# A recurrent layer in a four-layer model: elementwise steps on GpSimd, shared slots, output projections behind all blocks

## The chip, the cores and the metric

The kernel is one program on one core of a Trainium2 chip. A core has five engines that run side by side and wait for one another through semaphores: TensorE (PE: matrix products, with PEld for its weight loads), VectorE (DVE), ScalarE (ACT), GpSimd (POOL) and SyncE (SP, which issues the DMAs here). Each engine works through its own instructions strictly in the order in which they stand. The metric is the time of one execution in microseconds; less is better.

## The reference

The model has four layers; each is a mixer and an MLP, both followed by a layer normalization, on 256 tokens of 1024 channels in float32. Layers 0 and 3 mix by retention, layer 2 by latent attention, and layer 1 by the recurrence that the change is about:

```python
gate_branch, rec = jnp.split(x @ w_in, 2, axis=-1)          # 1024 -> 2 x 1280
gate_branch = jax.nn.gelu(gate_branch)
u = conv_general_dilated(rec, conv_w, ...) + conv_b         # 4 taps along the tokens
r = sigmoid(einsum(ub, w_a) + b_a); i = sigmoid(einsum(ub, w_x) + b_x)   # 10 blocks of 128 channels
log_a = -8 * r * softplus(-lam);  a = exp(log_a)
b_in = sqrt(-expm1(2 * log_a)) * (i * u)
h[t] = a[t] * h[t-1] + b_in[t]                              # a scan along the tokens
return (h * gate_branch) @ w_o                              # 1280 -> 1024
```

## The kernel before

Everything is kept transposed where it can be: channels on the 128 partitions, the 256 tokens along them. A float32 product is made of three products of float32r parts: a value is split into a high part (`hi`, a cast on ScalarE, line 140) and the rest (`lo`, a subtraction on VectorE, line 141). That holds for weights too: a chunk of 1 MB comes by DMA into a tile `raw` (3 slots) and is split into a tile `hl` (5 slots), so each chunk costs two casts of 128x1024 on ScalarE and two subtractions of that size on VectorE. `Feed` loads two chunks ahead of use.

The recurrent layer is the function `lru`. It treats its 1280 channels as five blocks `n` of 2x128. For each block:

- `block` and `rows` (TensorE) make the recurrent input in PSUM; `conv` (ScalarE line 569, VectorE line 571) makes `U[n]`, and its split `uT`.
- `gates(n)` multiplies by the gate weights, and ScalarE takes tanh and exp into `tr`, `ti` and `e0`, which have one slot each (lines 583 to 586): the next block's tanh can overwrite `ti` only when the readers of this block's are done. Four steps on VectorE follow: `B` (587), `Q` (588), `B` + 1 (589), `U` scaled by `ti` (590).
- `roots(n)` (line 604, ScalarE) takes the square root of `Q[n]`; all five stand together so that the activation table is loaded once.
- `scan(n)` (VectorE): `U*Q` (line 609), then two scans of 256 tokens (line 611), one for each 128 channels.
- `gate_branch(n)` (TensorE) makes the other half of the input product; `finish(n)` takes its gelu (ScalarE, 619), multiplies by the scan's result (VectorE, 620) and splits the product into `yT[n]` (lines 140 and 141).
- `out(n)` (line 155) multiplies `yT[n]` by a chunk of `w_o` into four PSUM accumulators.

The source before scans all five blocks, finishes blocks 0 and 1, issues `gate_branch` 3 and 4, then `out(0)`, `finish(2)`, `out(1)`, `finish(3)`, `finish(4)`; `close` makes `out` 2 to 4 and the layer normalization. The order on each engine is not that of the source: a scheduler goes over the instructions by priority and writes a fixed order for each engine, which the rows below the diff show. GpSimd does one thing in the kernel before: the power -0.5 of one column in `rstd` (line 162), 36 times.

Of the kernel before, what the change touches and what calls it, by code (L numbers as in the profile page):

```python
# [31 lines left out]
def constants():  # L32
    """Tables that depend on shapes alone."""
    c = {}
    c["c_idn"] = np.eye(128, dtype=np.float32)
    p = np.arange(128, dtype=np.float32)
    c["c_inv"] = np.stack(
        [np.float32(10000.0) ** (-p / np.float32(128)),
         np.float32(10000.0) ** (-(p % 32) / np.float32(32)),
         np.where((p // 32) % 2 == 0, -1.0, 1.0)], -1).astype(np.float32)  # L40
    j = np.arange(128, dtype=np.float64)[:, None]
    i = np.arange(256, dtype=np.float64)[None, :]
    dec = np.zeros((128, RH, 384), np.float64)
    for h in range(RH):
        lg = np.log1p(-np.exp2(-5.0 - h))
        full = np.where(i >= j, np.exp(lg * np.maximum(i - j, 0.0)), 0.0) * RDK ** -0.5
        dec[:, h, 128:] = full
        dec[:, h, :128] = full[:, :128]
    c["c_dec"] = dec.reshape(128, RH * 384).astype(np.float32)
    tri = np.where(np.arange(128)[None, :] <= np.arange(128)[:, None], 0.0, -1e30)  # L50
    c["c_msk"] = np.concatenate([np.zeros((128, 128)), tri, tri], 1).astype(np.float32)
    return c


def packed(w, k, n):
    """w [.., rows, cols] -> [.., rows / 128k, cols / n, 128, k, n]: each piece that is loaded at once in one stretch."""
    *b, r, c = w.shape
    w = w.reshape(*b, r // (128 * k), k, 128, c // n, n)
    m = len(b)
    return w.transpose(*range(m), m, m + 3, m + 2, m + 1, m + 4)  # L60


def laid_out(i):
    """The inputs as the kernel reads them; only the order of the weights' elements changes."""
    a = {n: i[n] for n in _PLAIN}
    w = i["ret_w_in"]
    a["ret_qk"] = packed(w[:, :, :2048], 8, 256)
    a["ret_vg"] = packed(w[:, :, 2048:], 4, 512)
    a["ret_o"] = packed(i["ret_w_o"], 2, 1024)
    a["lru_in"] = packed(i["lru_w_in"][0], 8, 256)  # L70
    a["lru_a"], a["lru_x"] = (i[n][0].transpose(1, 0, 2) for n in ("lru_w_a", "lru_w_x"))
    a["lru_o"] = packed(i["lru_w_o"][0], 2, 1024)
    a["mla_in"] = packed(i["mla_w_in"][0], 2, 704)
    a["mla_uq"] = packed(i["mla_w_uq"][0], 3, 384)
    a["mla_ukv"] = packed(i["mla_w_ukv"][0], 2, 1024)
    a["mla_o"] = packed(i["mla_w_o"][0], 2, 1024)
    w = i["mlp_w1"]
    a["mlp_1a"] = packed(w[:, :, :512], 4, 512)
    a["mlp_1b"] = packed(w[:, :, 512:], 8, 256)
    a["mlp_2"] = packed(i["mlp_w2"], 2, 1024)  # L80
    return {n: np.ascontiguousarray(x) for n, x in a.items()}


class Feed:
    """Weight tiles in the order of their use, each begun some tiles ahead of it."""

# [10 lines left out]
class Model:  # L97
# [13 lines left out]

# [1 line left out]
    def work(self):  # L113
# [6 lines left out]
    def chunk(self, src, k, n, pieces=2, loads=1, hold=True, mid=None):  # L120
        """src [128, k, n] in DRAM -> a tile [128, 2, k, n]: its high and low parts."""
        nc = self.nc
        raw = self.raw.tile([128, 2048], F32, name="raw", tag="raw")
        hl = self.hl.tile([128, 2, 2048], F32R, name="hl", tag="hl")
        w = k * n
        src = src.rearrange("p k n -> p (k n)")
        step = w // loads
        for a in range(0, w, step):
            nc.sync.dma_start(out=raw[:, a:a + step], in_=src[:, a:a + step])
            if mid and a == 0:  # L130
                mid()
        step = w // pieces
        for a in range(0, w, step):
            lo = self.split(hl[:, 0, a:a + step], hl[:, 1, a:a + step], raw[:, a:a + step])
            if hold and self.hold:
                self.after(lo, self.hold)
        return hl[:, :, :w].rearrange("p s (k n) -> p s k n", n=n)
# [5 lines left out]
    def mm3(self, out, st, mv, start, stop):  # L143
        """out += st @ mv with st, mv = (high, low)."""
        mm = self.nc.tensor.matmul
# [4 lines left out]
    def proj(self, acc, t, st, w, k, first, last, ns=(0, 1)):  # L150
        """acc[t] += st.T @ w[:, :, k]; st = (high, low) [128, 128 tokens], 1024 columns."""
        mm = self.nc.tensor.matmul
# [11 lines left out]

# [1 line left out]
    def setup(self):  # L166
# [23 lines left out]
    def vectors_load(self):  # L190
        """The vectors that are used by channel: rows of 128, turned into columns later."""
        nc, A = self.nc, self.A
# [100 lines left out]
    def close(self, acc, gb, final, emits, first=None):  # L293
        """The last products of a phase, each emit(t, ns), and its normalization.

        emits is for both token tiles, or for the second where first is for the other."""
        for t in range(2):
# [15 lines left out]
    def flush(self):  # L313
        """The second token tile of xT, after what the first alone allows."""
        if self.pending:
            self.hold = self.to_xT(1)
        self.pending = False

# [1 line left out]
    def rope2(self, p, ps, out):  # L320
        """ps [128, (x1 | x2), 256] in PSUM -> out [128, 2, (r1 | r2), 256], high and low."""
        nc = self.nc
# [8 lines left out]
    def ret(self, l, final, first=False):  # L331
# [4 lines left out]
        with tc.tile_pool(name="ret", bufs=1) as p:  # L336
# [25 lines left out]
            def begin():  # L362
                """The values of the first head, in the order in which the inputs arrive."""
                ps = [self.work() for t in range(2)]
# [123 lines left out]

# [1 line left out]
    def lru_setup(self, cols):  # L490
# [32 lines left out]
    def lru(self, l, final):  # L523
# [5 lines left out]
        with tc.tile_pool(name="lru", bufs=1) as p:  # L529
            UT, GB, YT = {}, {}, {}  # L530
            U = [p.tile([128, 2, 256], F32, name=f"U{n}") for n in range(5)]
            Q = [p.tile([128, 2, 256], F32, name=f"Q{n}") for n in range(5)]
            B = [p.tile([128, 2, 256], F32, name=f"B{n}") for n in range(5)]
            last = {}
# [40 lines left out]
            def gates(n, w, off):  # L575
# [11 lines left out]
                stt(out=B[n], in0=e0, scalar=1.0, in1=tr, op0=ALU.add, op1=ALU.mult)  # L587
                stt(out=Q[n], in0=B[n], scalar=2.0, in1=B[n], op0=ALU.add, op1=ALU.mult)
                nc.vector.tensor_scalar_add(out=B[n], in0=B[n], scalar1=1.0)
                stt(out=U[n], in0=ti, scalar=1.0, in1=U[n], op0=ALU.add, op1=ALU.mult)  # L590

# [16 lines left out]
            def scan(n):  # L608
                nc.vector.tensor_mul(out=U[n], in0=U[n], in1=Q[n])
                for b in range(2):  # L610
# [6 lines left out]
            def finish(n):  # L617
                g = p.tile([128, 2, 256], F32, name="gg", tag="gg", bufs=2)
                self.after(act(out=g, in_=GB[n], func=AF.Gelu_apprx_tanh), last["s"])
                nc.vector.tensor_mul(out=g, in0=g, in1=Q[n])  # L620
                YT[n] = p.tile([128, 2, 2, 256], F32R, name="yT", tag="yT", bufs=3)
                self.split(YT[n][:, 0], YT[n][:, 1], g)
# [39 lines left out]
            for n in range(5):  # L662
                roots(n)
            for n in range(5):
                scan(n)
                if n < 2:
                    finish(n)
            gate_branch(3, w)
            gate_branch(4, feed(("b", 4)))
            acc = self.accs()  # L670
            gb = self.ln_load(l, 0)
            for n in range(2):
                w = feed(("o", n))
                out(n, w, 0)
                out(n, w, 1)
                finish(n + 2)
            finish(4)
            self.close(acc, gb, final, [lambda t, ns, n=n: out(n, feed(("o", n)), t, ns) for n in (2, 3, 4)])

# [1 line left out]
    def mla(self, l, final):  # L681
# [6 lines left out]
        with tc.tile_pool(name="mla", bufs=1) as p:  # L688
# [13 lines left out]
            def down(t, i):  # L702
                """A latent of a token tile, normalized; with the first its rotary key."""
                c = slice(t * 128, t * 128 + 128)
# [34 lines left out]
            def tables():  # L739
                """Cosines and signed sines by token."""  # L740
                ps = self.work().rearrange("p (t a i) -> p t a i", t=2, a=2)
# [5 lines left out]
            def swapped(dst, src):  # L747
                """dst, src [128, k, r, 64]; the halves of the last axis trade places."""
                f = nc.scalar.copy if dst[1] == 0 else nc.vector.tensor_copy
# [3 lines left out]
            def rope(out, ps):  # L753
                """ps [128, (plain | swapped), 256] in PSUM."""
                a = p.tile([128, 2, 256], F32, name="ra", tag="ra")
# [25 lines left out]
            def q_load(n):  # L781
                """Columns of a pair of heads: (plain | swapped) rotary parts apart from the others."""
                raw = self.raw.tile([128, 2048], F32, name="raw", tag="raw")[:, :1152]
# [120 lines left out]

# [1 line left out]
    def mlp(self, l, final):  # L906
# [120 lines left out]
```

## Time and profile before

| | |
|---|---|
| median of 3 runs | 1343.36 us (1343.08 to 1346.11) |
| span of the profiled execution | 1343.4 us |
| TensorE busy | 1327.7 us, 99% |
| VectorE, ScalarE, GpSimd busy | 960.0, 663.8, 25.9 us |
| recurrent layer, first product to last | about 388 to 492 us of the span |

The profiled execution's span and the median of the runs are the same to 0.1 us, so nothing of note lies around the span. A busy TensorE is not a TensorE at its peak, but its products stand back to back; where it is idle is where time can be won, and where other engines can come to be waited for. The granted clock (PEclk) is given as a share of full speed.

### The profile page before, as it was taken

To read this page: it belongs to the slowest core of one execution; us is meant where nothing else is said; L and a number is where in the kernel's file an instruction comes from. 1 tells how busy PE (TensorE), PEld (TensorE's weight loads), DVE (VectorE), ACT (ScalarE), POOL (GpSimd) and SP (SyncE) were. 2 spreads that over 40 slices of the span, in tenths; PEclk is the share of its full clock that TensorE was granted. 3 is DMA by queue.
4 is the path that set the end of the run, shared out by engine and by line. 5 is a ranking of instruction groups with operands and counts; after the bars stand their busy time and mean duration, and the time that the engine had idled before them with its cause. 6 is when DMAs were issued, how large, how long until landed. Compare 5 with 4: busy or idle time off the path is not lost.

```text
span 1343.4 us, 18112 instructions
## 1 busy us (share of the span) xinstructions
PE 1327.7 (99%) x7184; PEld 1137.0 (85%) x7184; DVE 960.0 (71%) x1498; ACT 663.8 (49%) x1032; POOL 25.9 (2%) x40
## 2 busy tenths in 40 slices
PE   9999999999999999999999999999999999999997
PEld 7888888888889978888888888888898888888886
DVE  6986678666678988666688786666787657876664
ACT  5654345544438855444366454444354445454440
POOL 0000000000000000000000000000000000000000
PEclk9999999999999999999999999999999999999999
DMA  7754544655543456555354265555465444465530
GB/s 289 269 177 175 188 157 184 224 188 188 188 162 130 168 209 251 189 188 188 118 171 171 81 225 212 186 189 185 164 214 185 173 175 163 153 241 190 186 130 32
DMA packets 37426, 243.59 MB, mean 181 GB/s; under 512 B 4328, under 2 KB 4829, under 8 KB 10333
## 3 DMA queue, kind: packets, MB, share of 16 engines
q1 hardware_dynamic: 37340, 242.43, 50.4%
q8 instruction: 56, 0.92, 0.3%
q14 instruction: 30, 0.24, 0.1%
HBM read 241.36 MB, written 1.05 MB: 180 GB/s over the span
## 4 chain that ended last, share of the span: by engine, by line
PE 92%; DVE 4%; ACT 2%; issue 1%; DMA 0%; POOL 0%; SPq 0%; DVEq 0%; POOLq 0%; ACTq 0%
PE acc L155 36%; PE wk L933 14%; PE wk L146 11%; PE wk L148 10%; PE wk L147 10%; PE wk L934 7%; DVE hl L141 1%; PE wk L262 1%; ACT hl L140 1%; PE wk L424 1%; PE wk L955 0%; DVE Q L611 0%; ACT e L585 0%; DMA idn<-c_idn 0%; ACT tr L583 0%
## 5 line engine op out<-in xcount | busy, mean ns | idle before, releaser
L141 DVE TENSOR_TENSOR hl<-raw,hl 128x1024 fp32r<-128x1024 f32 (+2 forms) x450 | 523.1, 1192 | 196.7 <-ACT hl L140 193.6
L140 ACT CAST hl<-raw 128x1024 fp32r<-128x1024 f32 (+2 forms) x450 | 443.0, 1028 | 330.7 <-PE acc L155 191.9
L155 PE MATMUL acc<-hl,hT 128*128 128x512 f32 x1536 | 367.5, 395 | 0.0
L155 PEld LDWEIGHTS acc<-hl,hT 128*128 128x128 f32 x1536 | 285.4, 188 | 64.5
L933 PE MATMUL wk<-xT,hl 128*128 128x512 f32 x832 | 295.4, 398 | 0.0
L934 PE MATMUL wk<-xT,hl 128*128 128x256 f32 x832 | 233.3, 280 | 0.0
L933 PEld LDWEIGHTS wk<-xT,hl 128*128 128x128 f32 x832 | 156.3, 188 | 37.8
L146 PE MATMUL wk<-hl,xT 128*128 128x512 f32 (+1 forms) x432 | 158.8, 368 | 0.3 <-ACT xT L140 0.3
L934 PEld LDWEIGHTS wk<-xT,hl 128*128 128x128 f32 x832 | 157.1, 189 | 1.9
L148 PE MATMUL wk<-hl,xT 128*128 128x512 f32 (+1 forms) x432 | 157.3, 364 | 0.0
L147 PE MATMUL wk<-hl,xT 128*128 128x512 f32 (+1 forms) x432 | 157.1, 364 | 0.0
L155 PE MATMUL acc<-hl,yT 128*128 128x512 f32 x504 | 122.3, 400 | 2.5 <-ACT yT L140 2.2
L155 PEld LDWEIGHTS acc<-hl,yT 128*128 128x128 f32 x504 | 95.1, 191 | 26.3 <-ACT yT L140 2.7
L146 PEld LDWEIGHTS wk<-hl,xT 128*128 128x128 f32 x432 | 81.9, 190 | 14.7 <-ACT xT L140 2.6
L148 PEld LDWEIGHTS wk<-hl,xT 128*128 128x128 f32 x432 | 81.6, 189 | 14.0 <-DVE xT L141 1.6
L147 PEld LDWEIGHTS wk<-hl,xT 128*128 128x128 f32 x432 | 81.9, 190 | 12.9 <-DVE hl L141 1.0
L924 ACT COPY tb<-wk 128x256 f32<-128x256 f32 x104 | 38.8, 373 | 91.8 <-PE wk L934 91.8
L148 PE MATMUL wk<-xT,hl 128*128 128x256 f32 x288 | 81.6, 284 | 0.1
L146 PE MATMUL wk<-xT,hl 128*128 128x256 f32 x288 | 81.5, 283 | 0.0
L147 PE MATMUL wk<-xT,hl 128*128 128x256 f32 x288 | 81.4, 283 | 0.0
L925 DVE TENSOR_TENSOR s<-wk,tb 128x256 f32<-128x256 f32 x104 | 43.7, 420 | 45.6 <-ACT tb L924 45.5
L140 ACT CAST hT<-q 128x256 fp32r<-128x256 f32 x104 | 42.3, 407 | 50.7 <-DVE q L926 50.7
(218 smaller groups left out, 1391.8 us busy)
## 6 DMA issues: line engine op xcount, KB each, us to landing
raw<-mlp SPq DMA_DIRECT2D x64, 1024.0 KB, 4.8
raw<-mlp_1b SPq DMA_DIRECT2D x56, 1024.0 KB, 4.8
raw<-ret_vg SPq DMA_DIRECT2D x30, 1024.0 KB, 5.0
raw<-ret_qk SPq DMA_DIRECT2D x16, 1024.0 KB
raw<-ret_o SPq DMA_DIRECT2D x16, 1024.0 KB, 4.9
raw<-lru_in SPq DMA_DIRECT2D x10, 1024.0 KB, 4.8
raw<-mlp_1a SPq DMA_DIRECT2D x8, 1024.0 KB
raw<-lru_o SPq DMA_DIRECT2D x5, 1024.0 KB, 4.8
```

The costliest lines, as they stand in the source:

```text
L140: self.nc.scalar.copy(out=hi, in_=x)
L141: return self.nc.vector.tensor_sub(out=lo, in0=x, in1=hi.bitcast(F32))
L146: mm(out, lhsT=st[0], rhs=mv[0], start=start, stop=False)
L147: mm(out, lhsT=st[0], rhs=mv[1], start=False, stop=False)
L148: mm(out, lhsT=st[1], rhs=mv[0], start=False, stop=stop)
L155: mm(acc[t][n], lhsT=st[a], rhs=w[:, b, k, n * 512:n * 512 + 512], start=first and i == 0, stop=last and i == 2)
L262: nc.tensor.transpose(ps[:, k * 128:k * 128 + 128], self.h[t][:, (j * 4 + k) * 128:(j * 4 + k + 1) * 128], self.idn)
L424: nc.tensor.transpose(tp[:, b * 128:b * 128 + 128], Y[h, t][:, b * 128:b * 128 + 128], self.idn)
L924: nc.scalar.copy(out=tb, in_=ps_lo)
L925: nc.vector.tensor_add(out=s, in0=ps_hi, in1=tb)
L933: mm(ps, lhsT=w[:, 0, k, b * 128:b * 128 + 128], rhs=xT[:, k], start=k == 0, stop=False)
L934: mm(ps[:, 256:], lhsT=w[:, 1, k, b * 128:b * 128 + 128], rhs=xT[:, k, 0], start=False, stop=k == 7)
```

## The change

The steps on `Q`, `B`+1, `U` and the product `U*Q` go from VectorE to GpSimd. GpSimd has no combined step of two operations here, so what were four instructions on VectorE (588, 589, 590, 609) are six on GpSimd: `ti`+1, `U*ti`, `B`+2, `Q*B`, `B`+1, and `U*Q`. `U` and `B` become the two halves of one tile with the tag `UB` in five slots, and `yT` takes its slots from the same five. `finish` is called for all blocks before the first `out`. Docstrings and comments go too, which shifts line numbers by 3 in the second half of the file. The diff, cut to its code:

```diff
@@ lru @@
-            U = [p.tile([128, 2, 256], F32, name=f"U{n}") for n in range(5)]
+            UB = [p.tile([128, 2, 2, 256], F32, name="UB", tag="UB", bufs=5) for n in range(5)]
+            U, B = [x[:, 0] for x in UB], [x[:, 1] for x in UB]
             Q = [p.tile([128, 2, 256], F32, name=f"Q{n}") for n in range(5)]
-            B = [p.tile([128, 2, 256], F32, name=f"B{n}") for n in range(5)]
...
                 stt(out=B[n], in0=e0, scalar=1.0, in1=tr, op0=ALU.add, op1=ALU.mult)
-                stt(out=Q[n], in0=B[n], scalar=2.0, in1=B[n], op0=ALU.add, op1=ALU.mult)
-                nc.vector.tensor_scalar_add(out=B[n], in0=B[n], scalar1=1.0)
-                stt(out=U[n], in0=ti, scalar=1.0, in1=U[n], op0=ALU.add, op1=ALU.mult)
+                pool = nc.gpsimd
+                pool.tensor_scalar_add(out=Q[n], in0=B[n], scalar1=2.0)
+                pool.tensor_mul(out=Q[n], in0=Q[n], in1=B[n])
+                pool.tensor_scalar_add(out=ti, in0=ti, scalar1=1.0)
+                pool.tensor_mul(out=U[n], in0=U[n], in1=ti)
+                pool.tensor_scalar_add(out=B[n], in0=B[n], scalar1=1.0)
...
             def scan(n):
-                nc.vector.tensor_mul(out=U[n], in0=U[n], in1=Q[n])
+                nc.gpsimd.tensor_mul(out=U[n], in0=U[n], in1=Q[n])
...
-                YT[n] = p.tile([128, 2, 2, 256], F32R, name="yT", tag="yT", bufs=3)
+                YT[n] = p.tile([128, 2, 2, 256], F32R, name="yT", tag="UB", bufs=5)
...
-            for n in range(5):
+            for n in range(3):
                 scan(n)
-                if n < 2:
-                    finish(n)
+                finish(n)
             gate_branch(3, w)
             gate_branch(4, feed(("b", 4)))
+            for n in (3, 4):
+                scan(n)
+                finish(n)
             acc = self.accs()
             gb = self.ln_load(l, 0)
             for n in range(2):
                 w = feed(("o", n))
                 out(n, w, 0)
                 out(n, w, 1)
-                finish(n + 2)
-            finish(4)
```

On VectorE, at the end of the gates, before (`Q0` to `Q4`, `U0` to `U4` and `B0` to `B4` are the five blocks', the two `gg` are blocks 0 and 1):

```order
L589 TENSOR_SCALAR B4_3405<-B4_3405 128x512
L609 TENSOR_TENSOR U0_3391<-U0_3391,Q0_3396 128x512
L609 TENSOR_TENSOR U1_3392<-U1_3392,Q1_3397 128x512
L611 SCALAR_TENSOR_TENSOR Q0_3396<-B0_3401,U0_3391 128x256 x2
L611 SCALAR_TENSOR_TENSOR Q1_3397<-B1_3402,U1_3392 128x256 x2
L609 TENSOR_TENSOR U2_3393<-U2_3393,Q2_3398 128x512
L609 TENSOR_TENSOR U3_3394<-U3_3394,Q3_3399 128x512
L620 TENSOR_TENSOR gg_4143<-gg_4143,Q0_3396 128x512
L620 TENSOR_TENSOR gg_4152<-gg_4152,Q1_3397 128x512
L611 SCALAR_TENSOR_TENSOR Q2_3398<-B2_3403,U2_3393 128x256 x2
L141 TENSOR_TENSOR yT_4146<-gg_4143,yT_4146 128x512
L141 TENSOR_TENSOR yT_4155<-gg_4152,yT_4155 128x512
```

The same place of the changed kernel, where `UB_3391` to `UB_3395` hold `U` and `B` of blocks 0 to 4:

```order
L587 SCALAR_TENSOR_TENSOR UB_3395<-e0_4048,tr_4046 128x512
L141 TENSOR_TENSOR hl_4134<-raw_4133,hl_4134 128x1024 x2
L614 SCALAR_TENSOR_TENSOR Q0_3396<-UB_3391 128x256 x2
L614 SCALAR_TENSOR_TENSOR Q1_3397<-UB_3392 128x256 x2
L614 SCALAR_TENSOR_TENSOR Q2_3398<-UB_3393 128x256 x2
L614 SCALAR_TENSOR_TENSOR Q3_3399<-UB_3394 128x256 x2
L614 SCALAR_TENSOR_TENSOR Q4_3400<-UB_3395 128x256 x2
L623 TENSOR_TENSOR gg_4148<-gg_4148,Q0_3396 128x512
L623 TENSOR_TENSOR gg_4157<-gg_4157,Q1_3397 128x512
L141 TENSOR_TENSOR hl_4222<-raw_4221,hl_4222 128x1024
L141 TENSOR_TENSOR yT_4151<-gg_4148,yT_4151 128x512
L141 TENSOR_TENSOR yT_4160<-gg_4157,yT_4160 128x512
```

Before, the products for blocks 0 and 1 stand behind two blocks' scans; now they stand behind the scans of all five, and a weight chunk's subtraction stands between them and `yT`.

On GpSimd, in the same layer, the rows of the last block's gates and the five products (there are five rows like the first five for each of the blocks 0 to 3 ahead of these; before there is no row on GpSimd here):

```order
L591 TENSOR_SCALAR ti_4047<-ti_4047 128x512
L592 TENSOR_TENSOR UB_3395<-UB_3395,ti_4047 128x512
L589 TENSOR_SCALAR Q4_3400<-UB_3395 128x512
L590 TENSOR_TENSOR Q4_3400<-Q4_3400,UB_3395 128x512
L593 TENSOR_SCALAR UB_3395<-UB_3395 128x512
L612 TENSOR_TENSOR UB_3391<-UB_3391,Q0_3396 128x512
L612 TENSOR_TENSOR UB_3392<-UB_3392,Q1_3397 128x512
L612 TENSOR_TENSOR UB_3393<-UB_3393,Q2_3398 128x512
L612 TENSOR_TENSOR UB_3394<-UB_3394,Q3_3399 128x512
L612 TENSOR_TENSOR UB_3395<-UB_3395,Q4_3400 128x512
```

The first product of any block stands behind the gate steps of all of them. TensorE's order differs in the layer only in how the gate products are laid among the other blocks' products; SyncE's order is the same in both kernels.

## Rows read from the trace of the kernel before

**Rows 1.** Busy time of each engine, its share of the span, instructions (the page).
```profile
PE 1327.7 (99%) x7184; PEld 1137.0 (85%) x7184; DVE 960.0 (71%) x1498; ACT 663.8 (49%) x1032; POOL 25.9 (2%) x40
```

**Rows 2.** TensorE's waits in the whole span: us in total, times, longest.
```profile
PE acc L155 <- ACT yT L140: 2.2, 1, 2.2
PE wk L833 <- DVE s L828: 1.5, 1, 1.5
...
PE acc L155 <- DVE yT L141: 0.3, 1, 0.3
```

**Rows 3.** Busy time by stretch: PE, PEld, DVE, ACT, POOL, granted clock, DMA.
```profile
422.90:451.50 28.60, 28.60 (x241) 28.60 (x240) 27.10 (x43) 28.57 (x53) 0.00 (x0) 1.00 0.40 143
...
470.00:475.00 5.00, 2.76 (x12) 1.91 (x11) 4.42 (x6) 4.09 (x6) 0.00 (x0) 0.95 0.90 351
475.00:480.00 5.00, 5.00 (x17) 3.92 (x16) 3.20 (x5) 3.28 (x4) 0.00 (x0) 0.71 0.54 198
...
715.00:720.00 5.00, 3.53 (x31) 3.33 (x30) 4.62 (x12) 3.39 (x6) 0.00 (x0) 1.00 0.62 213
```

**Rows 4.** The chain that ended last, in the layer: start, us, what.
```profile
451.64 1.20 DVE U L609 x2
...
473.93 2.45 PE acc L155 x6
```

**Rows 5.** Timeline of TensorE: start, us, what, idle time before it and releaser.
```profile
458.01 1.09 PE L155 MATMUL acc<-hl,yT 128*128 128x512 f32 x4
459.40 12.29 PE L155 MATMUL acc<-hl,yT 128*128 128x512 f32 x51 [0.30 <-DVE yT L141]
473.93 6.24 PE L155 MATMUL acc<-hl,yT 128*128 128x512 f32 x19 [2.24 <-ACT yT L140]
```

**Rows 6.** Timeline of VectorE, last gates, products and scans.
```profile
447.75 0.68 DVE L587 SCALAR_TENSOR_TENSOR B<-e,tr 128x512 f32<-128x512 f32 x1
...
451.22 0.42 DVE L589 TENSOR_SCALAR B<-B 128x512 f32<-128x512 f32 x1
451.56 1.28 DVE L609 TENSOR_TENSOR U<-U,Q 128x512 f32<-128x512 f32 x2
452.76 2.42 DVE L611 TENSOR_TENSOR_SCAN Q<-B,U 128x256 f32<-128x256 f32 x4
...
456.29 1.28 DVE L620 TENSOR_TENSOR gg<-gg,Q 128x512 f32<-128x512 f32 x2
...
463.95 3.46 DVE L141 TENSOR_TENSOR hl<-raw,hl 128x1024 fp32r<-128x1024 f32 x3
```

**Rows 7.** Timeline of ScalarE: `ti` of the first and the last block, square roots.
```profile
422.43 0.46 ACT L584 ACTIVATE ti<-wk,half 128x256 f32<-128x256 f32 x1
...
442.94 0.49 ACT L584 ACTIVATE ti<-wk,half 128x256 f32<-128x256 f32 x1
...
444.64 0.50 ACT L584 ACTIVATE ti<-wk,half 128x256 f32<-128x256 f32 x1
...
450.26 2.71 ACT L604 ACTIVATE Q<-Q 128x512 f32<-128x512 f32 x5
```

**Rows 8.** Line 162 on GpSimd: ns min/median/max; then two of them with VectorE beside.
```profile
L162 POOL TENSOR_TENSOR rs<-ve,mhalf x36: 547/552/922, 58.1 to 1337.7; 128x1 f32<-128x1 f32 x36
...
57.97 0.74 DVE L415 SCALAR_TENSOR_TENSOR y<-wk,mv,g 128x512 f32<-128x512 f32 x1
58.13 0.55 POOL L162 TENSOR_TENSOR rs<-ve,mhalf 128x1 f32<-128x1 f32 x1 [57.69 <-DVE ve L161]
...
383.24 1.40 DVE L288 SCALAR_TENSOR_TENSOR h<-h,mv,lng 128x512 f32<-128x512 f32 x2
383.46 0.92 POOL L162 TENSOR_TENSOR rs<-ve,mhalf 128x1 f32<-128x1 f32 x1 [172.16 <-DVE ve L161]
```

**Rows 9.** One stretch, line 141 alone, then line 587 alone: DVE busy (count), clock, DMA.
```profile
422.90:451.50 28.60, 12.94 (x12) 1.00 0.40 143
...
422.90:451.50 28.60, 3.43 (x5) 1.00 0.40 143
```

## The prediction

> **What bounds the kernel now.** I read the busy times first: TensorE is busy 1327.7 us of 1343.4, the others far less [rows 1]. So over the whole span the time is TensorE's, and an edit on other engines can win only where TensorE waits for them. The second view is therefore TensorE's waits: in this layer they are two, 2.2 us for ScalarE's cast of `yT` and 0.3 us for VectorE's half of it [rows 2]. Its timeline puts them in place: the first output products start at 458.01, four of them run on high parts for 1.09 us, 0.30 us are lost at 459.1, then 51 products run, and 2.24 us are lost ahead of 473.93, where `yT` of block 2 is late [rows 5]. The windows show what follows the longer wait: the granted clock is 0.95 of full speed over 470 to 475 and 0.71 over 475 to 480 [rows 3], so (0.05 + 0.29) x 5 = 1.7 us more are lost. Waits of 2.54 us and 1.7 us of clock make 4.2 us, 0.3% of the time: that is all that can be won here.
>
> The chain that ended last says who is behind it: within the layer it runs through VectorE and ScalarE, not TensorE, from the products `U*Q` at 451.64 on, and comes back to TensorE at 473.93 [rows 4]. Over 422.9 to 451.5, the stretch of the gates, VectorE is busy 27.10 and ScalarE 28.57 of 28.60 us while TensorE never waits, and GpSimd does nothing [rows 3]. So the layer is balanced on three engines, with the elementwise chain just behind TensorE at its end.
>
> **The change part by part.** VectorE is relieved of `U*ti`, `Q`, `U*Q` at 0.60 us each (two in 1.28 with a tail of 0.08) and `B`+1 at 0.34 (451.22 to 451.56) [rows 6]: 3 x 0.60 + 0.34 = 2.14 us a block, 10.7 for five. It is worth nothing by itself if VectorE then waits for GpSimd's results, which is the question.
>
> *The price on GpSimd.* The trace before has no 128x512 step on GpSimd. Its nearest row is the power of one column, 0.55 us [rows 8], nearly all of it fixed cost. The lower end is VectorE's own 0.60 and 0.34 without a fixed part; the upper is 0.55 and VectorE's time twice, 1.75 and 1.23. I take once: 0.55 + 0.60 = 1.15 us for two inputs, 0.55 + 0.34 = 0.89 for one. A block's gates are three of the one and two of the other, 4.97 us; the five products come to 5.75.
>
> *Side by side with VectorE.* The power takes 0.55 us beside line 415, which reads one operand from PSUM, and 0.92 us beside line 288, which reads both from SBUF; the two shown stand for 20 and 16 of the 36 [rows 8]. So a GpSimd step that meets a VectorE step with two SBUF operands is 0.37 us late. Nearly all that VectorE does beside the new chain is of that kind: weight and `uT` subtractions of line 141, 12.94 us in the stretch, `B` of line 587, 3.43 us [rows 9], and then the scans. So I charge 0.37 us on each step: 1.52 and 1.26, a block 3 x 1.26 + 2 x 1.52 = 6.82 us. What a long GpSimd step does to VectorE no row shows; the forecast charges nothing for it, and the third rival below charges all of it.
>
> *The chain.* Block 0's `ti` is ready at 422.43 + 0.46 = 422.9, block 4's at 444.64 + 0.50 = 445.1 [rows 7]: a block each 5.56 us, which is less than 6.82, so GpSimd falls behind and is the bound from the first block on. Its gates end at 422.9 + 5 x 6.82 = 457.0. The products follow, since GpSimd's order has them behind all gates: 5 x 1.52 = 7.6, 464.6. The scans of the earlier blocks (0.6 us each) fit between; the last block's two add 1.2, 465.8. In the new order of VectorE the first `gg` stands behind all ten scans, then the second, a weight subtraction and `yT`: 0.60 + 0.60 + 1.15 (3.46 / 3 [rows 6]) + 0.68 = 3.03, so the lower part of block 0's `yT` is there at 468.8. TensorE reaches `out(0)` at 458.0 as before and can do four products on the high parts, to 459.1: it is idle 9.7 us.
>
> *What the wait holds up.* Behind that product stand all output products and, behind those, the layer normalization and everything after; nothing else of TensorE's can go ahead. The wait at 473.9 goes: 48 products of 12.29 / 51 = 0.24 us are 11.6 us between `out(0)` and `out(2)`, and VectorE has `yT` of block 2 ready some 5 us after that of block 0. The clock falls after the new wait as it did after the old one of 2.24 us; I set the two against each other (ends: nothing lost, 1.7 us won; twice lost, 1.7 us more).
>
> *`ti` has one slot.* Block 4's tanh into it can start only when GpSimd has scaled block 3's `U`: 422.9 + 3 x 6.82 + 1.26 + 1.52 = 446.1 against 442.94 now [rows 7]. ScalarE, full to 28.57 of 28.60 us, is pushed back by 3.2 us, and with it the casts of weights queued behind that tanh. What TensorE then waits for weights is taken off its wait for `yT`, since the chain on GpSimd is later still; the roots (450.26, then 453.5) remain ahead of the products (457.0). If GpSimd were quicker, this would not arise. The shared slots cost nothing: `yT` of a block reuses a tile whose last reader is that block's scan, and that scan already stands ahead on VectorE. SyncE's order is unchanged, and TensorE's instructions are the same in number.
>
> *The sum.* Idle before `out(0)` 9.7, less the 2.54 of before, is +7.2 us. The profiled span and the median of the runs agree to 0.1 us, so 1343.4 + 7.2 = 1350.6 us.
>
> **Rivals.**
>
> 1. *No mutual delay: not slower.* GpSimd keeps pace at 4.97 us a block. Block 4's `B` is ready at 447.75 + 0.68 = 448.4 [rows 6]; three steps of 2.93 us give 451.4, the products 457.1, the last scans 458.3, `yT` 461.3. TensorE is idle 2.2 us instead of 2.54: 1343.1, or 1341.4 if the clock then holds. The 0.37 us speak against it; that the delay was seen only for a step of one column, where VectorE lost nothing that the rows show, speaks for it. The point from which it decides: a block on GpSimd must cost under 5.56 us.
>
> 2. *GpSimd as quick as VectorE, and no delay: the best case.* Gates end at 448.4 + 1.28 = 449.7; the products wait for the roots, 450.26 + 0.61 = 450.9, then the ten scans bound: 451.5 + 6.0 + 3.03 = 460.5. Idle 1.4 us; a wait of 1.5 us elsewhere left the clock at 1.00 [rows 2, 3], so 2.54 - 1.4 + 1.7 = 2.8 us won, 1340.6. Even this is not 0.3%: what forbids more is the new order, in which ten scans stand ahead of the first `yT`. To win 4 us, `yT` would have to be ready by 459.
>
> 3. *Each waits for the other through the whole of a step.* Then GpSimd's gates, 24.9 us, and VectorE's steps with two SBUF operands in the stretch, 12.94 + 3.43 = 16.4, must follow one another: 422.9 + 41.2 = 464.1. Products and scans likewise: 5.75 + 6.0 = 11.75, to 475.9, and `yT` at 478.9. Idle 19.8: +17.3 us, 1360.7. The 0.37 us speak for it; nothing shows the reverse direction. On this the Trainium skill has a rule (SBUF — State Buffer, section on who interferes with whom): a VectorE step with two SBUF inputs and a GpSimd step that reads SBUF share one port, and whichever comes second stands still until the first is done. By that rule the time is this rival's; the rows show the one half of it, GpSimd's 0.92 us.
>
> 4. *A slower GpSimd.* At 1.75 and 1.23 us with no delay, a block costs 7.2: 458.9, products 467.6, `yT` 471.9, idle 12.8, +10.2, 1353.6. With the delay added 9.04 a block: 468.1, 478.7, 482.9, idle 23.8, +21.3, 1364.7.
>
> **How the numbers follow.** About 4.0 us (0.3%) is what a measurement of this kernel can tell from no change. The forecast, with the price and delay taken or rival 4's first variant, which lies beside it: 44%, own range 1347.5 to 1356. Rival 1: 20%, and rival 2: 7%, both within 0.3%, of which 4% in all go to faster by more for what the bounds may miss. Rival 3: 21%. Rival 4 with the delay: 8%. The range reaches from 1341.0, just under rival 1, to 1362.0, just above rival 3, and leaves out rival 2 and the slowest. Faster 0.04, within 0.3% 0.23, slower 0.73.
>
> **What would show it.** Right: GpSimd busy without a gap from about 423 to 464 with steps of 0.9 to 1.5 us; one wait of TensorE for `yT` of about 10 us, none ahead of `out(2)`; ScalarE waiting for GpSimd ahead of `ti`; the granted clock under 1 in the window behind the wait. A GpSimd that idles between blocks and a wait of 2 us would make rival 1 right. Line 141's 1.15 us stretched beside GpSimd, and gate steps that end at 464 and not 457, would make rival 3 right. It is wrong altogether if TensorE waits for weights inside the gate stretch by more than the 3 us that ScalarE's hold explains.

## The result, and the profile after

The changed kernel takes 1362.31 us (median of 4 runs, 1361.78 to 1363.51) against 1343.62 us (median of 4, 1343.08 to 1346.11) before: 1.0136 times as long [1.0124, 1.0148], 18.7 us slower. The forecast was 1350.6 us, with a range of 1341.0 to 1362.0. The sign and the chain were as forecast, the size was not.

The profiled execution of the changed kernel took 1361.78 us with a span of 1360.0. In every run on record that has both numbers, 27 of the kernel before among them, the time is 1.7 to 2.0 us above the span. So the profiled execution of the kernel before, whose span is 1343.4, took about 1345.2 us: within its runs, but above their median. That its span and the median of the runs agree to 0.1 us is chance; some 1.8 us lie around the span. Spans are therefore compared with spans below (+16.6 us), and times with times (+18.7 us).

Busy time of each engine, from the page after (it answers to [rows 1]):

```profile
PE 1329.5 (98%) x7184; PEld 1139.6 (84%) x7184; DVE 958.0 (70%) x1478; ACT 664.7 (49%) x1032; POOL 74.8 (5%) x70
```

VectorE lost 20 instructions but only 2.0 us of busy time, where the steps that left it had been priced at 10.7 us: what remains on it runs longer. GpSimd's 30 new steps took 48.9 us, 1.63 each. TensorE's waits in the whole span after (us in total, times, longest; beside [rows 2]):

```profile
PE acc L155 <- ACT yT L140: 13.6, 1, 13.6
PE wk L146 <- ACT uT L140: 3.8, 1, 3.8
PE wk L836 <- DVE s L831: 1.5, 1, 1.5
```

The 1.5 us elsewhere is as before. In the layer 2.54 us have become 17.4: one wait for `yT`, and a new one for `uT` in the middle of the gates. The timeline of TensorE after, at the first output product (beside [rows 5]):

```profile
478.18 26.65 PE L155 MATMUL acc<-hl,yT 128*128 128x512 f32 x108 [13.57 <-ACT yT L140]
```

Behind it 108 products run without another wait, so the wait ahead of `out(2)` is gone, as forecast. GpSimd's timeline after (start, us, what, idle before it), the first step of all, one of the second block, two of the fourth, the last gate step and the products:

```profile
422.36 1.50 POOL L591 TENSOR_SCALAR ti<-ti 128x512 f32<-128x512 f32 x1 [28.90 <-ACT ti L584]
...
432.38 2.40 POOL L592 TENSOR_TENSOR UB<-UB,ti 128x512 f32<-128x512 f32 x1
...
451.31 2.46 POOL L589 TENSOR_SCALAR Q<-UB 128x512 f32<-128x512 f32 x1
...
455.24 2.35 POOL L593 TENSOR_SCALAR UB<-UB 128x512 f32<-128x512 f32 x1
...
464.05 1.49 POOL L593 TENSOR_SCALAR UB<-UB 128x512 f32<-128x512 f32 x1
465.50 7.30 POOL L612 TENSOR_TENSOR UB<-UB,Q 128x512 f32<-128x512 f32 x5
```

GpSimd works from 422.4 to 472.8 almost without a gap. The gates end at 465.5 (forecast 457.0), and a one-input step takes 1.49 us at one place and 2.46 or 2.35 at another. VectorE's timeline after (beside [rows 6]):

```profile
447.95 1.10 DVE L587 SCALAR_TENSOR_TENSOR UB<-e,tr 128x512 f32<-128x512 f32 x1
448.97 3.45 DVE L141 TENSOR_TENSOR hl<-raw,hl 128x1024 fp32r<-128x1024 f32 x2
...
466.80 10.04 DVE L614 TENSOR_TENSOR_SCAN Q<-UB 128x256 f32<-128x256 f32 x10 [6.86 <-POOL UB L612]
476.76 1.26 DVE L623 TENSOR_TENSOR gg<-gg,Q 128x512 f32<-128x512 f32 x2
```

VectorE is slowed too: line 587 from 0.68 to 1.10 us, two weight subtractions from 2 x 1.15 to 3.45, ten scans from 6.0 to 10.04. ScalarE's timeline after (beside [rows 7]) shows the single slot of `ti`:

```profile
434.82 0.47 ACT L584 ACTIVATE ti<-wk,half 128x256 f32<-128x256 f32 x1 [2.82 <-POOL UB L592]
...
442.65 0.47 ACT L584 ACTIVATE ti<-wk,half 128x256 f32<-128x256 f32 x1 [1.39 <-POOL UB L592]
...
451.37 0.47 ACT L584 ACTIVATE ti<-wk,half 128x256 f32<-128x256 f32 x1 [1.75 <-POOL UB L592]
...
477.51 1.22 ACT L140 CAST yT<-gg 128x512 fp32r<-128x512 f32 x2 [9.56 <-DVE gg L623]
```

Three times the next tanh stands until GpSimd has scaled `U`; the cast of the fourth block's `uT` (437.38 after, 428.59 before), for which TensorE waits 3.8 us, is queued behind the first of them. The windows after (PE, PEld, DVE, ACT, POOL, granted clock, DMA; beside [rows 3]):

```profile
422.90:451.50 28.60, 24.80 (x187) 24.59 (x186) 18.51 (x25) 20.66 (x40) 27.11 (x18) 0.88 0.22 76
...
440.00:445.00 5.00, 5.00 (x31) 5.00 (x31) 1.87 (x3) 2.82 (x7) 4.83 (x4) 0.65 0.49 159
...
470.00:475.00 5.00, 0.00 (x0) 0.00 (x0) 5.00 (x6) 0.00 (x0) 2.80 (x2) 0.50 0.00 0
475.00:480.00 5.00, 1.82 (x4) 1.35 (x5) 5.00 (x9) 2.31 (x4) 0.00 (x0) 0.50 0.00 0
480.00:485.00 5.00, 5.00 (x21) 4.06 (x21) 5.00 (x8) 5.00 (x8) 0.00 (x0) 0.90 0.48 164
```

In the stretch of the gates ScalarE and VectorE are no longer full (20.66 and 18.51 where 28.57 and 27.10 stood): ScalarE waits for GpSimd, which is nearly full (27.11), and VectorE for ScalarE's casts (3.99 and 3.50 us at two of them). Behind the wait of 3.8 us TensorE works at a clock of 0.65 over 440 to 445 (0.50 over 438 to 442), though it is busy throughout. Behind the long wait the clock is 0.50, the lower level of 1.2 GHz, and is back to 0.90 in 480 to 485; most of that lower level lies where TensorE is idle anyway.

### The profile page after: what moved, and what is told of

Its sections match the earlier page's. It is cut to its first block, busy times and chain, and to the rows that moved or that the text cites. A ratio compares the mean times of both kernels' runs of the same rounds, so it can differ in the third digit from the quotient of the medians.

```text
span 1360.0 us, 18121 instructions
## 1 busy us (share of the span) xinstructions
PE 1329.5 (98%) x7184; PEld 1139.6 (84%) x7184; DVE 958.0 (70%) x1478; ACT 664.7 (49%) x1032; POOL 74.8 (5%) x70
## 4 chain that ended last, share of the span: by engine, by line
PE 92%; POOL 3%; DVE 2%; ACT 1%; DMA 1%; issue 0%; SPq 0%; DVEq 0%; POOLq 0%; ACTq 0%
PE acc L155 36%; PE wk L936 14%; PE wk L146 11%; PE wk L147 10%; PE wk L148 10%; PE wk L937 7%; PE wk L262 1%; DVE Q L614 1%; POOL UB L593 1%; POOL Q L589 1%; DVE hl L141 1%; DMA raw<-ret_qk 1%; POOL ti L591 1%; POOL UB L592 1%; PE wk L424 1%
## 5 line engine op out<-in xcount | busy, mean ns | idle before, releaser
L936 PEld LDWEIGHTS wk<-xT,hl 128*128 128x128 f32 x832 | 156.3, 188 | 37.8
L155 PE MATMUL acc<-hl,yT 128*128 128x512 f32 x504 | 121.4, 399 | 13.6 <-ACT yT L140 13.6
L162 POOL TENSOR_TENSOR rs<-ve,mhalf 128x1 f32<-128x1 f32 x36 | 26.0, 723 | 1249.5 <-DVE ve L161 1249.5
L146 PEld LDWEIGHTS wk<-hl,xT 128*128 128x128 f32 x432 | 81.8, 189 | 14.7 <-ACT xT L140 2.6
```

Of the source, the lines that this page charges most:

```text
L146: mm(out, lhsT=st[0], rhs=mv[0], start=start, stop=False)
L155: mm(acc[t][n], lhsT=st[a], rhs=w[:, b, k, n * 512:n * 512 + 512], start=first and i == 0, stop=last and i == 2)
L162: nc.gpsimd.tensor_tensor(out=r, in0=v, in1=self.mhalf[:, :n], op=ALU.pow)
L936: mm(ps, lhsT=w[:, 0, k, b * 128:b * 128 + 128], rhs=xT[:, k], start=k == 0, stop=False)
```

## The experiments

Two theories were put to the test. The expectations call them *port* and *price*. Port: GpSimd and VectorE keep each other out while both read two operands from SBUF, so both become slower. Price: GpSimd's steps are simply dearer than forecast, wherever they stand. A third possibility is that the order of `finish` and the slots cost the time, not GpSimd.

**The steps by themselves.** A small program of its own, which computes nothing of the model, repeats the steps at 128x512: 12 on VectorE, 6 on GpSimd, each alone and then side by side. Its five kinds of step, one line for each:

```diff
+ v_tt: nc.vector.tensor_mul(out=o, in0=a, in1=b)          # L43, both operands in SBUF
+ v_ps: nc.vector.tensor_mul(out=o, in0=s, in1=b)          # L47, s in PSUM
+ v_ts: nc.vector.tensor_scalar_add(out=o, in0=b, scalar1=1.0)   # L51
+ g_tt: nc.gpsimd.tensor_mul(out=o, in0=a, in1=b)          # L55
+ g_ts: nc.gpsimd.tensor_scalar_add(out=o, in0=a, scalar1=1.0)   # L59
```

> A program of its own that computes none of the model: steps of 128x512 in sections that follow one another, six on GpSimd and twelve on VectorE, first each alone, then side by side, VectorE once with both operands in SBUF and once with one in PSUM. Theory price (GpSimd's steps are simply long): alone 1.29 us for two inputs and 1.49 for one, as the undisturbed steps of the changed kernel, and the same beside either VectorE step. Theory port (each stands still while the other reads two operands from SBUF): beside VectorE's steps with both operands in SBUF, six GpSimd steps of 1.3 and twelve VectorE steps of 0.6 take 6 x 1.3 + 12 x 0.6 = 15 us together, and beside those with one operand in PSUM the longer of the two, some 8 us. Theory independence: 8 us in both sections.

VectorE's timeline (the first three rows alone, then beside L55, L55 and L59):

```profile
5.43 7.31 DVE L43 TENSOR_TENSOR vo<-a,b 128x512 f32<-128x512 f32 x12 [0.35 <-ACT b L39]
13.24 7.27 DVE L47 TENSOR_TENSOR vo<-s,b 128x512 f32<-128x512 f32 x12 [0.50 <-ACT b L39]
20.86 4.12 DVE L51 TENSOR_SCALAR vo<-b 128x512 f32<-128x512 f32 x12 [0.35 <-ACT b L39]
42.31 13.71 DVE L43 TENSOR_TENSOR vo<-a,b 128x512 f32<-128x512 f32 x12 [17.33 <-ACT a L38]
56.53 7.27 DVE L47 TENSOR_TENSOR vo<-s,b 128x512 f32<-128x512 f32 x12 [0.52 <-ACT b L39]
64.48 9.71 DVE L43 TENSOR_TENSOR vo<-a,b 128x512 f32<-128x512 f32 x12 [0.68 <-ACT b L39]
```

GpSimd's timeline (the first two rows alone, then the three that stand beside the last three above):

```profile
25.43 7.36 POOL L55 TENSOR_TENSOR po<-a,b 128x512 f32<-128x512 f32 x6 [25.01 <-ACT b L39]
33.29 8.77 POOL L59 TENSOR_SCALAR po<-a 128x512 f32<-128x512 f32 x6 [0.49 <-ACT b L39]
42.36 10.10 POOL L55 TENSOR_TENSOR po<-a,b 128x512 f32<-128x512 f32 x6 [0.31 <-ACT a L38]
56.65 7.39 POOL L55 TENSOR_TENSOR po<-a,b 128x512 f32<-128x512 f32 x6 [4.19 <-ACT b L39]
64.35 9.57 POOL L59 TENSOR_SCALAR po<-a 128x512 f32<-128x512 f32 x6 [0.31 <-ACT b L37]
```

Alone, a two-input step of GpSimd costs 7.36 / 6 = 1.22 us and a one-input step 8.77 / 6 = 1.46: the step with less to read is the dearer one, and both ends that the prediction gave for it (0.34 and 1.23) lie below. Side by side with both operands in SBUF, VectorE's 12 steps take 13.71 us; one after the other all 18 would be 7.31 + 7.36 = 14.7. GpSimd's six take 10.10 us for 7.36. With one of VectorE's operands in PSUM both run as if alone (7.27 and 7.39, and 7.27 and 8.77 with GpSimd's one-input steps). The one-input step holds VectorE up by (9.71 - 7.31) / 6 = 0.40 us of its 1.46. A last section was to set it beside VectorE's one-input steps, but these began only when GpSimd was done, so it shows nothing. The mutual delay is thus shown, and so is a dear one-input step. The rule that the third rival cited (Trainium skill, SBUF — State Buffer, section on who interferes with whom) is borne out in who meets whom: two SBUF operands on VectorE clash, one in PSUM does not. That the second stands still until the first's whole instruction is done is nearly so for two inputs, and not so for one.

**Order and slots alone.** All steps go back to VectorE; the order of `finish` and the shared slots stay.

```diff
-                pool.tensor_scalar_add(out=Q[n], in0=B[n], scalar1=2.0)
...
+                stt(out=Q[n], in0=B[n], scalar=2.0, in1=B[n], op0=ALU.add, op1=ALU.mult)
+                nc.vector.tensor_scalar_add(out=B[n], in0=B[n], scalar1=1.0)
+                stt(out=U[n], in0=ti, scalar=1.0, in1=U[n], op0=ALU.add, op1=ALU.mult)
...
-                nc.gpsimd.tensor_mul(out=U[n], in0=U[n], in1=Q[n])
+                nc.vector.tensor_mul(out=U[n], in0=U[n], in1=Q[n])
```

> The changed kernel with all steps back on VectorE: only the shared slots and the order (output projections behind all blocks) are left of the change. Theory GpSimd (price or port): the order costs little. On VectorE five products of 0.6 and ten scans of 0.6 from 451.6 give 460.6, the first yT 3.0 later at 463.6; TensorE is idle about 4.5 us at once instead of 2.5 in two pieces: 1344 to 1346 us. Rival, order: most of the 18.7 us come from scans that all stand ahead of the first yT: 1355 us or more.

1342.43 us (11 runs) against 1344.87 (15 runs) before: 0.9985 [0.9977, 0.9994]. That is below the expectation, and the fastest kernel of this study: 2.4 us under the kernel before. This is less than the 4.0 us that the prediction took as what a measurement can tell, but the two sets of runs do not overlap (at most 1343.05, at least 1343.1). VectorE's timeline, then TensorE's waits in this layer from 420 on:

```profile
454.50 2.43 DVE L611 TENSOR_TENSOR_SCAN Q<-UB 128x256 f32<-128x256 f32 x4
456.85 1.26 DVE L620 TENSOR_TENSOR gg<-gg,Q 128x512 f32<-128x512 f32 x2
```

```profile
PE acc L155 <- DVE yT L141: 1.1, 1, 1.1
PE acc L155 <- DVE hl L141: 0.2, 1, 0.2
```

The prediction held that the new order sets ten scans ahead of the first `yT`. That is so only with the products on GpSimd: with them on VectorE the scheduler puts the two `gg` behind the third block's scans, at 456.85. TensorE waits 1.3 us in these rows, 2.54 before, and the granted clock stays at 1.00 in every window from 455 to 480, where 0.95 and 0.71 stood [rows 3]. So order and slots are a small gain by themselves; the loss is GpSimd's.

**GpSimd alone.** The kernel before, with nothing changed but the steps that go to GpSimd.

```diff
-                stt(out=Q[n], in0=B[n], scalar=2.0, in1=B[n], op0=ALU.add, op1=ALU.mult)
...
+                pool.tensor_scalar_add(out=Q[n], in0=B[n], scalar1=2.0)
...
             def scan(n):
-                nc.vector.tensor_mul(out=U[n], in0=U[n], in1=Q[n])
+                nc.gpsimd.tensor_mul(out=U[n], in0=U[n], in1=Q[n])
```

> The kernel before with the steps moved to GpSimd and nothing else: own tiles for U and B, three yT slots, finish of blocks 2 to 4 between the output products. Theory GpSimd: gates on GpSimd end near 465.5 as in the changed kernel; the first yT needs two products and two scans less than all five, so it can be some 6 us earlier, but a later wait for yT comes back: 1355 to 1361 us. Rival, order: under 1348 us.

1362.38 us (4 runs), 1.0130 [1.0116, 1.0144], a little over what was expected and not to be told from the changed kernel's 1.0136. TensorE's waits from 420 on:

```profile
PE acc L155 <- ACT yT L140: 11.9, 1, 11.9
PE wk L146 <- ACT uT L140: 5.1, 1, 5.1
PE wk L147 <- DVE uT L141: 0.4, 1, 0.4
```

The same two waits and a short third one, 17.4 us in all. On VectorE ten scans stand in one piece ahead of the first `gg` here too (from 467.13, 10.04 us), though the source has the old order. The move to GpSimd makes the whole loss, and the better order gives nothing back where GpSimd is late.

**The product back on VectorE.** The changed kernel, with `U*Q` alone on VectorE again.

```diff
-                nc.gpsimd.tensor_mul(out=U[n], in0=U[n], in1=Q[n])
+                nc.vector.tensor_mul(out=U[n], in0=U[n], in1=Q[n])
```

> The changed kernel with the product U*Q alone back on VectorE; the gates stay on GpSimd. They end near 465.5 as in the changed kernel. Of the products and scans those of blocks 0 to 3 are then done before, so that behind 465.5 stand one root (0.6), one product (0.6), two scans (1.2) and 3.0 up to yT: 471, against 479.7 in the changed kernel. Theory price and port (five products on GpSimd and ten scans shut each other out at the end): 1353 to 1356 us. Rival, gates alone (the end does not matter, since the gates are late anyway): 1360 us or more.

1355.21 us (4 runs), 1.0078 [1.0064, 1.0091], as expected. TensorE's wait for `yT` falls from 13.6 to 4.8 us; that for `uT` stays at 3.8. The gates end at 466.0, against 465.5 in the changed kernel. So the products on GpSimd, behind the gates, are worth 7.1 us, and the gates by themselves 12.8 (1355.21 less the 1342.43 of the same order with all steps on VectorE).

**The product alone on GpSimd.** The other half: the changed kernel with its gate steps back on VectorE, so that only `U*Q` is on GpSimd.

```diff
-                pool.tensor_scalar_add(out=Q[n], in0=B[n], scalar1=2.0)
...
+                stt(out=Q[n], in0=B[n], scalar=2.0, in1=B[n], op0=ALU.add, op1=ALU.mult)
...
```

> The kernel with order and slots of the change and all gate steps on VectorE; only the product U*Q on GpSimd. VectorE is through with the gates at 451.6 as before. Theory price (1.22 us a product, scans untouched, two scans of 0.6 behind each): products end at 457.7, the last scans at 458.9, yT at 461.9: 1341 to 1343 us, no slower than with the product on VectorE (1342.4). Theory port: products and scans one after the other, 5 x 1.22 + 10 x 0.6 = 12.1, 463.7, yT at 466.7, idle 7.6 us and the clock falls: 1347 to 1350 us.

1348.32 us (8 runs), 1.0026 [1.0016, 1.0036]: inside what port gave, above what price gave. GpSimd's timeline, then VectorE's:

```profile
451.08 7.64 POOL L609 TENSOR_TENSOR UB<-UB,Q 128x512 f32<-128x512 f32 x5 [57.38 <-ACT Q L604]
```

```profile
451.17 1.49 DVE L589 TENSOR_SCALAR UB<-UB 128x512 f32<-128x512 f32 x1
452.59 10.17 DVE L611 TENSOR_TENSOR_SCAN Q<-UB 128x256 f32<-128x256 f32 x10
```

Five products take 7.64 us where five alone would be 5 x 1.22 = 6.1, and ten scans 10.17 where ten alone are 6.0. Even `B`+1 on VectorE, one input, takes 1.49 us for 0.42 [rows 6]. The products begin 7 us before TensorE comes to the outputs at 458, and it still waits 5.9 us for `yT`. The loss of 3.3 us against the kernel before hides the gain from order and slots: against the same order with all steps on VectorE (1342.43) the products cost 5.9 us, not much less than the 7.1 behind late gates. With that order the medians are thus 1342.43 with nothing on GpSimd, +5.9 with the products, +12.8 with the gates and +19.9 with both: the two parts make 18.7 of the 19.9. (The kernel before stood at 1343.6 to 1345.0 beside these runs, so a difference of 1 us says nothing.)

**The one-input steps back on VectorE.** The changed kernel, with the three adds on VectorE.

```diff
-                pool.tensor_scalar_add(out=Q[n], in0=B[n], scalar1=2.0)
+                nc.vector.tensor_scalar_add(out=Q[n], in0=B[n], scalar1=2.0)
...
-                pool.tensor_scalar_add(out=ti, in0=ti, scalar1=1.0)
+                nc.vector.tensor_scalar_add(out=ti, in0=ti, scalar1=1.0)
...
-                pool.tensor_scalar_add(out=B[n], in0=B[n], scalar1=1.0)
+                nc.vector.tensor_scalar_add(out=B[n], in0=B[n], scalar1=1.0)
```

> The changed kernel with the three one-input additions of each block on VectorE (0.34 us each); GpSimd keeps the three products. Theory price: GpSimd's gates cost 2 x 1.38 = 2.8 us a block, less than the 5.6 us in which blocks come, so it keeps up; five products of 1.38 from 450.3 end at 457.2, scans at 458.4, yT at 461.4: TensorE idle 2.3 us, 1342 to 1344 us. Theory port: products and scans follow one another, 5 x 1.3 + 10 x 0.6 = 12.5 us, 462.8, yT at 465.8, idle 6.7 us: 1347 to 1350 us.

1354.79 us (5 runs), 1.0074 [1.0060, 1.0088]: slower than either theory gave. GpSimd's timeline:

```profile
445.50 2.21 POOL L590 TENSOR_TENSOR Q<-Q,UB 128x512 f32<-128x512 f32 x1 [1.69 <-DVE Q L589]
449.72 2.21 POOL L592 TENSOR_TENSOR UB<-UB,ti 128x512 f32<-128x512 f32 x1 [2.01 <-DVE ti L591]
454.04 2.21 POOL L590 TENSOR_TENSOR Q<-Q,UB 128x512 f32<-128x512 f32 x1 [2.10 <-DVE Q L589]
```

GpSimd now has two steps a block and stands idle before each until VectorE has done an add, which waits in VectorE's queue behind other work: ahead of the last two of these rows behind a weight subtraction, ahead of the first behind a subtraction of `uT` and the step of line 587. The handing to and fro takes the place of the dear steps: from one block's line 592 to the next it is still 6.4 to 7.2 us, and these three steps meet a weight subtraction besides (2.21 us for 1.22). Neither theory had this term, so the run doesn't part them: it says only that the adds are worth 7.5 us net of the handing over.

**No clash with the weights' subtractions.** The changed kernel, with the layer's weight chunks' low parts written by a VectorE memset, which reads nothing, in place of the subtraction of two operands.

```diff
+        if light:
+            return self.nc.vector.memset(lo.bitcast(F32), 0.0)
...
-                return self.chunk(win[o + n], 8, 256, hold=hold)
+                return self.chunk(win[o + n], 8, 256, hold=hold, light=True)
...
-                return self.chunk(wo[n], 2, 1024)
+                return self.chunk(wo[n], 2, 1024, light=True)
```

> The changed kernel, but the low parts of the recurrent layer's input and output weights (all but the gate weights) are set to zero by a fill on VectorE instead of the subtraction that reads two operands from SBUF: it leaves out the low part of those weights, and VectorE has two-operand steps from SBUF beside GpSimd only for uT, B and the scans. Theory price: GpSimd's steps are as long as in the changed kernel (a block 8.3 to 10 us, gates to 465): 1360 us or more. Theory port: the gate steps stay at their undisturbed 1.29 and 1.49, a block 7.5 us, gates end at 460, and only the products clash with the scans: 1353 to 1357 us.

1358.23 us (4 runs), 1.0099 [1.0084, 1.0115]: between the two theories. GpSimd's timeline, one whole block, then the products (the line numbers are 2 higher):

```profile
430.76 1.49 POOL L593 TENSOR_SCALAR ti<-ti 128x512 f32<-128x512 f32 x1
432.33 1.29 POOL L594 TENSOR_TENSOR UB<-UB,ti 128x512 f32<-128x512 f32 x1
433.60 1.49 POOL L591 TENSOR_SCALAR Q<-UB 128x512 f32<-128x512 f32 x1
435.17 1.26 POOL L592 TENSOR_TENSOR Q<-Q,UB 128x512 f32<-128x512 f32 x1
436.52 1.49 POOL L595 TENSOR_SCALAR UB<-UB 128x512 f32<-128x512 f32 x1
437.98 1.66 POOL L593 TENSOR_SCALAR ti<-ti 128x512 f32<-128x512 f32 x1
...
460.50 7.40 POOL L614 TENSOR_TENSOR UB<-UB,Q 128x512 f32<-128x512 f32 x5
```

A block in which no step is stretched takes 437.98 - 430.76 = 7.22 us: 4.60 in the three one-input steps (1.57, 1.57, 1.46 from start to start) and 2.62 in the two others. Beside it VectorE does little: two memsets, steps that read PSUM, and from 436.87 on a subtraction of `uT` and the step on the next `B`, beside which the step on GpSimd stays at 1.49. By the small program the five steps would take 3 x 1.46 + 2 x 1.22 = 6.8 us; in the kernel a step that needs the one before starts some 0.08 us later. The gates end at 460.5, 37.8 us after their start, against 43.1: the subtractions cost the gates 5.3 us, and of what is left 5 x 7.22 = 36.1 is price. That the memset is also shorter than the subtraction explains none of it, since GpSimd's gates wait for VectorE only 0.64 us in the changed kernel. The scans, not touched by the edit, still take 10.11 us. This run settles the shares: most of the gates' length is price, a smaller part of it exclusion, and what the scans lose is exclusion.

## Why the prediction was wrong

**What bounds the kernel, and the chain: right.** TensorE lost nothing of its own; it waited at the one product that was named, for the chain that was named. GpSimd was the bound from block 1 on, ScalarE stood for `ti`, the wait ahead of `out(2)` went. The chain that ended last, after (beside [rows 4]):

```profile
466.80 6.07 DVE Q L614 x4
478.18 26.65 PE acc L155 x108
```

**The price on GpSimd: the step that failed.** The forecast took 0.89 us for a one-input step and 1.15 for one of two inputs. In the block without a stretched step they cost 4.60 / 3 = 1.53 and 2.62 / 2 = 1.31, start to start. The second was near; the first was 0.64 too low, and above even the upper end of 1.23. Both ends had been scaled from VectorE, on which fewer inputs are quicker (0.34 and 0.61 us), the upper with the fixed cost of a one-column step. On GpSimd the ratio is the other way round, which no row before could show. The term: 5 x (7.22 - 4.97) = 11.3 us, of which 5 x (4.60 - 2.67) = 9.7 are the one-input steps.

**Side by side with VectorE: half right.** The 0.37 us charged on each step came to 9.3 us for the gates; measured are 43.1 - 5 x 7.22 = 7.0. So GpSimd's own delay was sized well in the sum, which is partly luck: the three longest steps, each beside weight subtractions, are 1.10 (432.38), 0.97 (451.31) and 0.86 us late (455.24), and others stand at 1.49 and 1.29 as in the block above. That the forecast charges nothing to VectorE was wrong: the last scans ended 4.0 us behind the last product, where 1.2 was forecast, since the scans had to share their time with five products. Line 614 in ns, min/median/max:

```profile
L614 DVE TENSOR_TENSOR_SCAN Q<-UB x10: 656/658/1737, 466.8 to 476.2; 128x256 f32<-128x256 f32 x10
```

The first four scans, while products run, start 1.60 to 1.66 us apart; the other six take 0.6 each, as before.

The sum, from the forecast's +7.2 to the measured +16.5 at the end of the layer (its first transposes, before and after):

```profile
488.17 1.03 PE L262 MATMUL wk<-idn,h 128*128 128x128 f32 x8
504.67 1.03 PE L262 MATMUL wk<-idn,h 128*128 128x128 f32 x8
```

| step of the forecast | forecast | measured | us |
|---|---|---|---|
| first gate step starts | 422.9 | 422.36 | -0.5 |
| five blocks, price | 24.9 | 36.1 | +11.3 |
| five blocks, delay | 9.3 | 7.0 | -2.3 |
| five products | 7.6 | 7.3 | -0.3 |
| last product to last scan | 1.2 | 4.0 | +2.8 |
| last scan to first output product | 3.0 | 1.3 | -1.7 |
| four products ahead of the wait | 1.1 | 0 | +1.1 |
| output products up to the transposes, waits left out, after less before | 0 | -1.1 | -1.1 |

These add up to +9.3 and give 16.5. The last scan is sooner followed by TensorE because its first product needs only the high part of `yT`, and the lower part came in time. The four products ahead of the wait were a slip of the forecast: the high part, too, is a cast of `gg`, and so stands behind the ten scans; none could run at 458. The last row: from the first output product to the transposes it is 488.17 - 458.01 less the waits of 2.54, or 27.6 us, before [rows 5], and 504.67 - 478.18 = 26.5 after, for 109 and 108 products. The clock explains little of it: 1.7 us were lost to it before, and after 0.50 x 1.82 over 475 to 480 and 0.10 x 5 over 480 to 485, or 1.4. What else made these products quicker stays open.

**`ti` has one slot: right in kind, wrong in place and size.** The hold was forecast for the last block's tanh, as 3.2 us; that tanh starts at 451.37 and not 442.94, 8.4 us later. TensorE's wait came earlier than forecast and was not for weights: behind the third block's tanh (434.82, before 431.36) the cast of the fourth block's `uT` was late. That its 3.8 us are near 3.2 is chance. It was indeed taken off the later wait. At 464.6 TensorE came to the outputs, 6.6 us later than at 458.0: the 3.8, and 2.8 lost at the lower clock behind it (0.50 x 1.96 over 438 to 440 and 0.35 x 5 over 440 to 445 make 2.7). Since the chain on GpSimd ended later still, this cost nothing in the end.

**The rivals.** The third forecast 1360.7 us, and its steps lie near what was measured: gates end at 464.1 (465.5), scans at 475.9 (476.8). Its mechanism is real, but its sum is not confirmed by that: it had 24.9 us of steps and 16.4 of exclusion, and measured are 36.1 and 7.0. Two errors offset each other. Its exclusion was too strict because the one-input step holds VectorE up for 0.40 us only, as the small program shows. The truth is the fourth rival's dearer GpSimd with a weaker form of the third's mutual delay. With the delay the fourth gave 1364.7 us at 9.04 us a block (8.6), but it had the two prices the wrong way round: 1.75 for two inputs and 1.23 for one, where 1.31 and 1.53 were measured. The first two are excluded: a block needed under 5.56 us, and 8.6 is what it took.

**Open.** In the small program a one-input step of GpSimd lost 0.13 us beside VectorE's steps of 0.61 us; in the kernel it lost 0.97 beside steps of 1.2 us. Which length or order of issue makes the difference was not tried. Nor was a combined step of two operations tried on GpSimd; that it has none there is how the change is written, and no run shows more. The spread of the kernel before (1343.08 to 1346.54 us over all its runs) was not looked into either; 2.1 us of the 18.7 lie between spans and medians and are not in the table.

## What to carry to other kernels

Price a step on an engine that has never run it by measuring that step on that engine, one form at a time; an upper end scaled from another engine is no bound. Moving elementwise work from a busy VectorE to an idle GpSimd relieved little here, where both read two SBUF operands (2.0 us of the 10.7), and it made the slower engine the end of the chain; when both have to run, let VectorE read an operand from PSUM or do its two-operand work at another time. When a change comes in parts, run the parts apart: here the order and the slots were a small gain, hidden under a loss several times as large.

## What the runs showed of the hardware that was not expected

- On GpSimd an add of a constant to 128x512 costs 1.46 us and a product of two such tiles 1.22; on VectorE 0.34 and 0.61. The Trainium skill (GPSIMD Engine Reference, section on engine selection) says of GpSimd that "1-input is roughly line-rate"; these rows don't agree: the one-input step is the dearer of the two there, and takes four times as long as on VectorE.
- The exclusion goes both ways, and scans take part in it: 1.60 to 1.66 us from start to start beside GpSimd's products, 0.60 alone.
- An operand in PSUM took VectorE out of it altogether: 7.27 us for 12 steps, alone and beside either kind of GpSimd's steps.
- A wait of 3.8 us in mid-stretch was followed by a granted clock of 0.65 over 440 to 445, with TensorE busy throughout: 2.8 us lost behind it (6.6 us late at the outputs, less the 3.8), where the forecast had priced only the clock behind the wait for `yT`.
